# Hybrid encoder block on one core: the attention probabilities of two heads transposed in one step, with the products' PSUM bank as second target

## The chip, the cores and the metric

The kernel runs on one core of one Trainium2 chip. The time is the device time of one execution in microseconds (us). In the profile PE is TensorE, DVE VectorE, ACT ScalarE, POOL GpSimd and SP the engine that issues most of the DMAs; a head here is an attention head.

## The reference, cut to what matters

Two layers work on 256 tokens with 1024 channels in float32. A layer is a feed-forward half, a mixing half and a second feed-forward half. The mixing half projects the tokens once, runs two kinds of attention with eight heads each ("na" over a neighbourhood on a grid, "sw" over a sliding window with a learned sink), gates both and projects them back.

```python
for l in range(DEPTH):                                     # DEPTH = 2
    x = x + 0.5 * swiglu(rms_norm(x, ffn1_norm[l]), ...)
    z = rms_norm(x, mix_norm[l]) @ w_in[l]                 # q, k, v of both kinds, two gates
    o_na = neighbourhood_attention(qa, ka, va, na_rpb[l])  # 8 heads x 64
    o_sw = sliding_window_gqa(qs, ks_, vs, t5_bias, sw_sink[l])
    merged = g[:, :, 0] * (o_na @ w_branch_na[l]) + g[:, :, 1] * (o_sw @ w_branch_sw[l])
    x = x + merged @ w_out[l]
    x = x + 0.5 * swiglu(rms_norm(x, ffn2_norm[l]), ...)
# each kind of attention, for every head:
#   s = q k^T / 8 + bias (masked);  p = softmax(s);  o = p v
```

## The kernel before

Weights come through a ring of 512 KB pieces, and the float32 products are made of three fast matmuls: each operand is split into a rounded high part and a remainder, ScalarE writing the high part (line 184) and VectorE the remainder (line 185). For weights these are wh and wl, for probabilities ph and pl. Lines 170 to 172 are the three matmuls; one of them has 512 columns.

TensorE's order is the order of the program's text; the other engines' orders are set by a scheduler at build time that works with a modelled timeline, with a priority raised by 500 for the attention steps. Within the mixing half the heads' work is laid between the matmuls of the projections. A clock of the program (`now`, `tick`) counts 1 for three 512-column matmuls; `defer(lag, ...)` puts a step off until that clock has gone on by `lag`, and `need` calls it early where its result is wanted. A head goes through three such steps:

- `front(h)`: four matmuls make the scores (tile sc); VectorE adds the bias and finds the maximum (line 571); ScalarE takes the exponentials (line 574); VectorE sums and inverts (lines 579 and 580); GpSimd scales the rows (line 581). The rows are the tile S.
- `turn(h, S_)`, `P_LAG` = 10 after it (more for a few heads, by `MORE`): four transposes of 128x128 write the PSUM tile pt (line 589); ScalarE and VectorE split it into ph and pl.
- `back(h, ph, pl)`, `V_LAG` = 7.5 after that: four matmuls of 256 columns multiply the split probabilities with the values into one half of the PSUM tile po, which two heads share (line 603). ScalarE reads part of that half (line 607) and VectorE adds the rest (line 608) into the tile o; after the odd head o is split into oB (sw) or oA (na).

The tiles pt and po have one bank each, sc has two. S has `LAG` = 3 buffers, ph and pl have 2 each. The sixteen heads of a layer follow each other, first the eight of sw and then the eight of na; below they are called sw 0 to 7 and na 0 to 7. The gates (line 655) and the local and grid projections (lines 703 to 741) run beside the last heads.

Of the kernel before, what the change touches and what calls it, by code (L numbers as in the profile page):

```python
# [11 lines left out]
F32 = mybir.dt.float32  # L12
F32R = mybir.dt.float32r
# [8 lines left out]
P = 128  # L22
# [4 lines left out]
T = S // P  # L27
# [12 lines left out]
NEG = -1e30  # L40
RING = 6
RAW = 4
LAG = 3
H_LAG, NORM_LAG, QK_LAG, P_LAG, V_LAG, M_LAG = 7.9, 4.0, 16, 10, 7.5, 5.5
LAST_LAG = 6.1
MORE = {"Q1": 2, ("sw", 4): 1.5, ("na", 4): 2, ("na", 5): 1.5}
# [12 lines left out]
def hybrid_encoder(ctx, tc, x, w_gu1, w_d1, w_in, b_gate, qk_gain, rpb, sink, t5,  # L59
                   w_bna, w_bsw, w_out, w_gu2, w_d2, c_mask, c_band, out):  # L60
    nc = tc.nc
# [6 lines left out]
    ps_acc = ctx.enter_context(tc.tile_pool(name="ps_acc", bufs=1, space=PSUM))  # L68
# [19 lines left out]
    ident = const.tile([P, P], F32, name="ident")  # L88
# [35 lines left out]
    def linked(engine, emit):  # L124
        with ExitStack() as order:
            if engine in chain:
                order.enter_context(tc.issue_after(chain[engine].ins))
            inst = emit()
        if chain:
            chain[engine] = inst  # L130
        return inst
# [23 lines left out]
    def defer(lag, key, fn):  # L155
        later.append((now[0] + lag, len(later), key, fn))
        later.sort(key=lambda e: e[0])

    def need(*keys):
        for e in [e for e in later if e[2] in keys]:  # L160
            later.remove(e)
            e[3]()
# [16 lines left out]
    def flipped(ap):  # L179
        step, n = ap.ap[-1]  # L180
        return bass.AP(tensor=ap.tensor, offset=ap.offset + step * (n - 1), ap=[*ap.ap[:-1], [-step, n]])

    def split_to(hi, lo, src):
        linked("act", lambda: nc.scalar.activation(hi, src, AF.Copy))  # L184
        linked("dve", lambda: nc.vector.tensor_tensor(lo, src, hi.bitcast(F32), ALU.subtract))  # L185
# [301 lines left out]
    def mix(l, n, after):  # L487
        with tc.tile_pool(name="mix", bufs=1) as mp:
# [52 lines left out]
            def attend(name, ins, qT, kh, kl, kidx, bias_of, vcol, ready, oT, sink_l=None):  # L541
                oh, ol = oT
                po = [None, None]
                with tc.issue_after(rstd_done[0].ins):
                    bias = [bias_of(0), bias_of(1)]

                def urgent(fn):
                    def run(*args):
                        with tc.high_priority(500):
                            fn(*args)  # L550
                    return run

                @urgent
                def front(h):
                    need(*ins)
                    if h + 2 < NH:
                        bias.append(bias_of(h + 2))
                    b = bias.pop(0)
                    least = FMAX
                    if sink_l is not None:  # L560
                        sk, least = (v[:, sink_l * NH + h:sink_l * NH + h + 1] for v in (snk, nsnk))
                    ps = ps_acc.tile([P, T, S], F32, name="sc", tag="sc", bufs=2)
                    S_ = mp.tile([P, T, S], F32, name="S", tag="S", bufs=LAG)
                    mx = small.tile([P, T], F32, name="mx", tag="mx")
                    sm = small.tile([P, T], F32, name="sm", tag="sm")
                    for t in range(T):
                        for i, k in enumerate((kh, kl)):
                            nc.tensor.matmul(ps[:, t, :], qT[:, h, t * P:(t + 1) * P], k[:, kidx(h), :],  # L568
                                             start=i == 0, stop=i == 1)
                    for t in range(T):  # L570
                        nc.vector.tensor_tensor_reduce(S_[:, t, :], ps[:, t, :], b(t), -1.0, least,  # L571
                                                       ALU.add, ALU.min, mx[:, t:t + 1])
                    for t in range(T):
                        nc.scalar.activation(S_[:, t, :], S_[:, t, :], AF.Exp, bias=mx[:, t:t + 1], scale=-1.0,  # L574
                                             accum_out=sm[:, t:t + 1])
                    if sink_l is not None:
                        es = small.tile([P, T], F32, name="es", tag="es")
                        nc.scalar.activation(es, mx, AF.Exp, bias=sk)
                        nc.vector.tensor_tensor(sm, sm, es, ALU.add)
                    nc.vector.reciprocal(sm, sm)  # L580
                    nc.gpsimd.tensor_tensor(S_, S_, sm.unsqueeze(2).to_broadcast([P, T, S]), ALU.mult)  # L581
                    defer(P_LAG + MORE.get((name, h), 0), (name, h, 0), lambda: turn(h, S_))

                @urgent
                def turn(h, S_):
                    tp = ps_acc.tile([P, T, T, P], F32, name="pt", tag="pt")
                    for t in range(T):
                        for kt in range(T):
                            nc.tensor.transpose(tp[:, kt, t, :], S_[:, t, kt * P:(kt + 1) * P], ident)  # L589
                    ph = mp.tile([P, T, T, P], F32R, name="ph", tag="ph", bufs=2)  # L590
                    pl = mp.tile([P, T, T, P], F32R, name="pl", tag="pl", bufs=2)
                    split_to(ph, pl, tp)
                    defer(V_LAG, (name, h, 1), lambda: back(h, ph, pl))

                @urgent
                def back(h, ph, pl):
                    assert ready()
                    if h % 2 == 0:
                        po[0] = ps_acc.tile([P, 2, T, P], F32, name="po", tag="po")
                        po[1] = mp.tile([P, T, P], F32, name="o", tag="o", bufs=2)  # L600
                    for kt in range(T):
                        for i, p in enumerate((ph, pl)):
                            nc.tensor.matmul(po[0][:, h % 2], vcol(kt, h), p[:, kt], start=kt + i == 0,  # L603
                                             stop=kt + i == 2)
                    a, b = (0, DH) if h % 2 == 0 else (DH, 0)
                    o, ov = po[1], flipped(po[0][:, h % 2])
                    nc.scalar.activation(o[a:a + DH], ov[b:b + DH], AF.Copy)
                    nc.vector.tensor_tensor(o[a:a + DH], o[a:a + DH], ov[a:a + DH], ALU.add)
                    if h % 2:
                        split_to(oh[:, h // 2], ol[:, h // 2], o)  # L610

                for h in range(NH):
                    yield lambda h=h: front(h)
# [49 lines left out]
            def na_bias(h):  # L663
                t2 = mp.tile([P, T2W], F32, name="t2", tag="t2", bufs=2)
                for r in range(2):
# [10 lines left out]
                return lambda t: b[:, t].rearrange("p r c -> p (r c)")  # L676

            sw = attend("sw", ("Q0", "Q1", "K0", "K1"), sqT, *skT, lambda h: h // 4, sw_bias,
                        lambda kt, h: sv[:, kt, h // 4, h % 2 * DH:h % 2 * DH + P], lambda: True, oB, sink_l=l)
            na = attend("na", ("q0", "q1", "k0", "k1"), qT, *kT, lambda h: h, na_bias,  # L680
                        lambda kt, h: va[:, kt, h, :], lambda: "v1" in done, oA)
            step = {
# [8 lines left out]
            heads = iter([*[(sw, h) for h in range(NH)], *[(na, h) for h in range(NH)]])  # L691
            due = 0
            for token in ORDER.split():
                if token[0] == "a":
                    it, h = next(heads)
# [149 lines left out]
```

## Time and profile before

| | us |
|---|---|
| median of three runs (1076.62 to 1077.98) | 1076.77 |
| the profiled execution | 1076.94 |
| its span, first to last instruction | 1075.2 |

In the profile's groups, a row gives the line, the engine, the operation, what is written and read, how often, then the busy time in us and the mean of one in ns. In a list by time, a row gives the start and the length in us. The length of a matmul includes its way through the array, and matmuls overlap; what one costs is the distance from its start to the next start. The PE clock is TensorE's granted clock as a share of full speed; it was 0.999 over the span.

### The profile page before, as it was taken

Reading aid. Unit: us, or ns where it says so; the run is one execution under the profiler, and the core shown is the slowest. Engines: PE = TensorE matmul, PEld = TensorE weight load, DVE = VectorE, ACT = ScalarE, POOL = GpSimd, SP = SyncE. Lnnn points to the kernel's source line nnn. Section 1 sums busy time; section 2 is a strip of 40 time slices with the busy share of each in tenths; the row PEclk is TensorE's granted clock in tenths of the full one; section 3 lists DMA queues with packets and bytes.
Section 4 is the critical chain, followed back from the end, with each engine's and each line's share of the span. In section 5 each row is a group of like instructions: output and inputs, shape, how many; then the busy total and the mean of one; then the engine's idle time right before and its main releaser. Section 6 shows DMA issues by size and latency. Waiting matters only on the chain.

```text
span 1075.2 us, 14749 instructions
## 1 busy us (share of the span) xinstructions
PE 1068.2 (99%) x5125; PEld 890.3 (83%) x5125; DVE 875.8 (81%) x1337; ACT 671.5 (62%) x1014; POOL 116.7 (11%) x118
## 2 busy tenths in 40 slices
PE   8999999999999999999999999999999999999998
PEld 6888888888888888888888888888888888888887
DVE  6678799889886768869977887988898867778696
ACT  6566654788764556565565665557877646566552
POOL 1000120243520000000000000003534000000000
PEclk9999999999999999999999999999999999999999
DMA  7767656765654667756657765657666554776652
GB/s 247 227 214 237 215 190 191 228 194 155 192 188 137 198 199 246 242 168 191 214 162 238 227 213 185 199 153 247 177 195 185 176 175 160 237 231 203 188 196 89
DMA packets 98827, 212.63 MB, mean 198 GB/s; under 512 B 7568, under 2 KB 13744, under 8 KB 98752
## 3 DMA queue, kind: packets, MB, share of 16 engines
q1 hardware_dynamic: 98560, 211.60, 62.3%
q8 instruction: 40, 0.66, 0.2%
q14 instruction: 35, 0.29, 0.1%
q0 software_dynamic: 192, 0.08, 0.1%
HBM read 210.59 MB, written 1.06 MB: 197 GB/s over the span
## 4 chain that ended last, share of the span: by engine, by line
PE 97%; DMA 1%; ACT 1%; DVE 0%; issue 0%; SPq 0%; ACTq 0%
PE g L170 22%; PE g L172 22%; PE g L171 22%; PE acc L170 5%; PE acc L172 5%; PE acc L171 5%; PE tp L320 2%; PE sc L568 1%; PE po L603 1%; PE tp L170 1%; PE tp L171 1%; PE tp L172 1%; PE pt L589 1%; PE tp L201 1%; PE br L170 1%; PE br L171 1%
## 5 line engine op out<-in xcount | busy, mean ns | idle before, releaser
L185 DVE TENSOR_TENSOR wl<-raw,wh 128x1024 fp32r<-128x1024 f32 x336 | 405.7, 1219 | 65.5 <-ACT wh L184 61.8
L184 ACT ACTIVATE wh<-raw 128x1024 fp32r<-128x1024 f32 x336 | 346.7, 1045 | 117.3 <-DMA raw<-in_w_gu 51.4
L170 PE MATMUL g<-wh,xh 128*128 128x512 f32 (+1 forms) x976 | 383.1, 393 | 0.5 <-DVE hh L444 0.5
L172 PE MATMUL g<-wh,xl 128*128 128x512 f32 (+1 forms) x976 | 377.8, 387 | 0.0
L171 PE MATMUL g<-wl,xh 128*128 128x512 f32 (+1 forms) x976 | 377.5, 387 | 0.0
L172 PEld LDWEIGHTS g<-wh,xl 128*128 128x128 f32 x976 | 183.4, 188 | 39.1 <-DVE xl L185 1.5
L170 PEld LDWEIGHTS g<-wh,xh 128*128 128x128 f32 x976 | 183.6, 188 | 33.8 <-DVE hh L444 1.1
L171 PEld LDWEIGHTS g<-wl,xh 128*128 128x128 f32 x976 | 183.7, 188 | 33.4 <-DVE wl L185 0.6
L443 ACT ACTIVATE sg<-g,rs_y 128x256 f32<-128x256 f32 x88 | 41.1, 467 | 89.7 <-PE g L172 77.3
L444 DVE SCALAR_TENSOR_TENSOR hh<-g,rs_y,sg 128x256 f32<-128x256 f32 x88 | 42.3, 481 | 53.0 <-ACT sg L443 53.0
L170 PE MATMUL acc<-wh,hi 128*128 128x512 f32 x180 | 71.2, 395 | 0.0
L171 PE MATMUL acc<-wl,hi 128*128 128x512 f32 x180 | 70.2, 390 | 0.0
L172 PE MATMUL acc<-wh,lo 128*128 128x512 f32 x180 | 70.1, 390 | 0.0
L176 POOL TENSOR_TENSOR rs_y<-ms,mhalf 128x1 f32<-128x1 f32 x12 | 8.1, 678 | 556.5 <-DVE ms L222 548.0
L352 DVE TENSOR_TENSOR u<-raw 128x512 f32<-128x512 f32 x64 | 41.7, 686 | 20.9 <-DMA raw<-in_w_d 20.8
L184 ACT ACTIVATE corner<-raw 128x512 fp32r<-128x512 f32 x32 | 20.1, 629 | 40.4 <-DMA raw<-in_w_d 22.4
L581 POOL TENSOR_TENSOR S<-S,sm 128x512 f32<-128x512 f32 x32 | 37.2, 1161 | 65.6 <-DVE sm L580 38.3
L172 PEld LDWEIGHTS acc<-wh,lo 128*128 128x128 f32 x180 | 33.8, 188 | 7.2
L171 PEld LDWEIGHTS acc<-wl,hi 128*128 128x128 f32 x180 | 33.8, 188 | 6.7
L170 PEld LDWEIGHTS acc<-wh,hi 128*128 128x128 f32 x180 | 33.8, 188 | 6.7
L184 ACT ACTIVATE wh<-v 128x1024 fp32r<-128x1024 f32 x20 | 21.2, 1062 | 28.9 <-DVE v L352 24.5
L574 ACT ACTIVATE S<-S,mx 128x256 f32<-128x256 f32 x64 | 31.9, 499 | 8.0 <-DVE mx L571 7.9
(189 smaller groups left out, 1522.0 us busy)
## 6 DMA issues: line engine op xcount, KB each, us to landing
raw<-in_w_gu SPq DMA_DIRECT2D x176, 512.0 KB, 4.5
raw<-in_w_d SPq DMA_DIRECT2D x100, 512.0 KB, 4.2
raw<-in_w_in SPq DMA_DIRECT2D x64, 512.0 KB, 4.7
raw<-in_w_out SPq DMA_DIRECT2D x16, 512.0 KB, 3.6
bb<-in_b_gate SPq DMA_DIRECT2D x16, 256.0 KB, 3.6
raw<-in_w_bsw SPq DMA_DIRECT2D x8, 512.0 KB, 3.9
raw<-in_w_bna SPq DMA_DIRECT2D x8, 512.0 KB, 3.5
raw<-in_w_d SPq DMA_DIRECT2D x12, 256.0 KB, 2.7
```

The source lines that it names most:

```text
L170: nc.tensor.matmul(ps, xh, wh, start=first, stop=False)
L171: nc.tensor.matmul(ps, xh, wl, start=False, stop=False)
L172: nc.tensor.matmul(ps, xl, wh, start=False, stop=last)
L184: linked("act", lambda: nc.scalar.activation(hi, src, AF.Copy))
L185: linked("dve", lambda: nc.vector.tensor_tensor(lo, src, hi.bitcast(F32), ALU.subtract))
L201: nc.tensor.transpose(tp[:, i, :], xs[t][:, k * P:(k + 1) * P], ident)
L320: nc.tensor.transpose(tp[:, SLOT[t][i], :], hh[:, t, i * P:(i + 1) * P], ident)
L352: sub = lambda to, x, y: nc.vector.tensor_tensor(to, x, y, ALU.subtract)
L443: linked("act", lambda: nc.scalar.activation(sg, ps[:, :FC], AF.Silu, scale=rstd[t]))
L444: linked("dve", lambda: nc.vector.scalar_tensor_tensor(pair[0][:, t], ps[:, FC:], rstd[t], sg, op0=ALU.mult, op1=ALU.mult))
L574: nc.scalar.activation(S_[:, t, :], S_[:, t, :], AF.Exp, bias=mx[:, t:t + 1], scale=-1.0, accum_out=sm[:, t:t + 1])
L581: nc.gpsimd.tensor_tensor(S_, S_, sm.unsqueeze(2).to_broadcast([P, T, S]), ALU.mult)
```

## The change

Two heads are turned together. `front` keeps its head in a list, and only the odd head defers a turn, with its own lag. That turn transposes both heads: the even one into a tile with the tag po (the bank of the values' products), the odd one into pt. Both are then split, and one deferred step multiplies both with the values, the even head first. S has five buffers in place of three.

```diff
-LAG = 3
+LAG = 5
...
+                held = []
...
-                    defer(P_LAG + MORE.get((name, h), 0), (name, h, 0), lambda: turn(h, S_))
+                    held.append((h, S_))
+                    if h % 2:
+                        pair_, held[:] = list(held), []
+                        defer(P_LAG + MORE.get((name, h), 0), (name, h, 0), lambda: turn(pair_))
 
                 @urgent
-                def turn(h, S_):
-                    tp = ps_acc.tile([P, T, T, P], F32, name="pt", tag="pt")
-                    for t in range(T):
-                        for kt in range(T):
-                            nc.tensor.transpose(tp[:, kt, t, :], S_[:, t, kt * P:(kt + 1) * P], ident)
-                    ph = mp.tile([P, T, T, P], F32R, name="ph", tag="ph", bufs=2)
-                    pl = mp.tile([P, T, T, P], F32R, name="pl", tag="pl", bufs=2)
-                    split_to(ph, pl, tp)
-                    defer(V_LAG, (name, h, 1), lambda: back(h, ph, pl))
+                def turn(heads):
+                    tps = [ps_acc.tile([P, T, T, P], F32, name="pt", tag=tag) for tag in ("po", "pt")]
+                    for (_, S_), tp in zip(heads, tps):
+                        for t in range(T):
+                            for kt in range(T):
+                                nc.tensor.transpose(tp[:, kt, t, :], S_[:, t, kt * P:(kt + 1) * P], ident)
+                    ready_ = []
+                    for (h, _), tp in zip(heads, tps):
+                        ph = mp.tile([P, T, T, P], F32R, name="ph", tag="ph", bufs=2)
+                        pl = mp.tile([P, T, T, P], F32R, name="pl", tag="pl", bufs=2)
+                        split_to(ph, pl, tp)
+                        ready_.append((h, ph, pl))
+                    defer(V_LAG, (name, heads[1][0], 1), lambda: [back(*r) for r in ready_])
```

In the changed file the lines from `held = []` on have moved: the turn's transposes are line 594, the products line 611, ScalarE's and VectorE's reads of po lines 615 and 616, the scores line 569, the reductions 572, the exponentials 575 and the gates 663. In the orders below a row gives the line, the operation, the tiles and sizes, and in brackets the engines that it waits for; DVE is VectorE, Activation ScalarE and Pool GpSimd.

TensorE in layer 1, before: the products of head sw 3, six matmuls of a gate's projection, and the turn of head sw 5.

```order
L603 MATMUL po<-ph,sv 128x256 [waits DVE_49]
L603 MATMUL po<-pl,sv 128x256
L603 MATMUL po<-ph,sv 128x256
L603 MATMUL po<-pl,sv 128x256
L170 MATMUL g<-wh,xh_1793 128x512
L171 MATMUL g<-wl,xh_1793 128x512
L172 MATMUL g<-wh,xl_1794 128x512
L170 MATMUL g<-wh,xh_1793 128x512
L171 MATMUL g<-wl,xh_1793 128x512
L172 MATMUL g<-wh,xl_1794 128x512
L589 MATMUL pt<-ident,S 128x128 [waits DVE_49,PE_49,Pool_49]
L589 MATMUL pt<-ident,S 128x128
```

After, at the same place: the products of head sw 3 (those of sw 2 stand just ahead), six matmuls, and the turn of heads sw 4 and 5.

```order
L611 MATMUL po<-ph,sv 128x256 [waits DVE_49]
L611 MATMUL po<-pl,sv 128x256
L611 MATMUL po<-ph,sv 128x256
L611 MATMUL po<-pl,sv 128x256
L170 MATMUL g<-wh,xh_1793 128x512
L171 MATMUL g<-wl,xh_1793 128x512
L172 MATMUL g<-wh,xl_1794 128x512
L170 MATMUL g<-wh,xh_1793 128x512
L171 MATMUL g<-wl,xh_1793 128x512
L172 MATMUL g<-wh,xl_1794 128x512
L594 MATMUL pt<-ident,S 128x128 [waits DVE_49,Pool_49]
L594 MATMUL pt<-ident,S 128x128 x3
```

The products of two heads now stand together, and the first transposes behind them write the bank that these products wrote; the wait for VectorE there is for its last read of that bank. Before, it was for the remainder pl of the turn before.

ScalarE, after, around the products of heads sw 4 and 5: both reads of po (line 615) stand around the two exponentials of head na 0.

```order
L664 ACTIVATE gate_1821<-gate_1821 128x512 [waits DVE_49]
L615 ACTIVATE o<-po 64x256 [waits PE_49]
L575 ACTIVATE S,sm<-S,mx 128x256 [waits DVE_49,Pool_49]
L575 ACTIVATE S,sm<-S,mx 128x256 [waits DVE_49]
L615 ACTIVATE o<-po 64x256 [waits DVE_49,PE_49]
```

The second of the two reads waits for VectorE as well as for TensorE: VectorE's read of the even head's half comes first.

VectorE at the end of the attention stage, before: the reads of po for heads na 4 and na 5 (line 608) stand apart among the splits of the weights, two wl ahead of the first and two between them.

```order
L185 TENSOR_TENSOR wl<-raw,wh 128x1024 [waits DMAHW0_49,Activation_49]
L185 TENSOR_TENSOR wl<-raw,wh 128x1024 [waits DMAHW1_49,Activation_49]
L608 TENSOR_TENSOR o<-o,po 64x256 [waits Activation_49]
L185 TENSOR_TENSOR wl<-raw,wh 128x1024 [waits DMAHW2_49,Activation_49]
L185 TENSOR_TENSOR pl<-pt,ph 128x512 [waits Activation_49]
L655 SCALAR_TENSOR_TENSOR gate_1822<-g,rs_y,bb 128x512 [waits DMAHW5_49,PE_49]
L185 TENSOR_TENSOR wl<-raw,wh 128x1024 [waits DMAHW4_49,Activation_49]
L608 TENSOR_TENSOR o<-o,po 64x256 [waits Activation_49]
```

After, at the same place:

```order
L185 TENSOR_TENSOR wl<-raw,wh 128x1024 [waits DMAHW0_49,Activation_49]
L185 TENSOR_TENSOR wl<-raw,wh 128x1024 [waits DMAHW1_49,Activation_49]
L185 TENSOR_TENSOR wl<-raw,wh 128x1024 [waits DMAHW2_49,Activation_49]
L663 SCALAR_TENSOR_TENSOR gate_1822<-g,rs_y,bb 128x512 [waits DMAHW5_49,PE_49]
L185 TENSOR_TENSOR wl<-raw,wh 128x1024 [waits DMAHW4_49,Activation_49]
L616 TENSOR_TENSOR o<-o,po 64x256 [waits Activation_49] x2
```

Both reads now come behind all four wl and the gate; a split of probabilities has gone from between them, since both heads' splits stand earlier.

## The prediction

> **What bounds the kernel now.** I read the page first (busy shares), then the table by stretches over the two attention stages, then what TensorE waited for, and last the instructions in order of time around a few heads.
>
> ```profile
> span 1075.2 us, 14749 instructions
> PE 1068.2 (99%) x5125; PEld 890.3 (83%) x5125; DVE 875.8 (81%) x1337; ACT 671.5 (62%) x1014; POOL 116.7 (11%) x118
> ```
> ```profile
> core 0: us, PE busy (x) PEld busy (x) DVE busy (x) ACT busy (x) POOL busy (x), PEclk, DMA share, GB/s
> 224.00:325.00 101.00, 101.00 (x554) 86.06 (x553) 87.64 (x187) 78.65 (x167) 37.84 (x29) 1.00 0.61 184
> 755.00:856.00 101.00, 101.00 (x554) 86.05 (x553) 87.76 (x186) 78.63 (x168) 37.83 (x29) 1.00 0.61 184
> ```
> ```profile
> PE idle L120 <- DVE blank L115: 1.6, 1, 1.6
> PE tp L201 <- DMA x<-in_x: 1.3, 1, 1.3
> PE g L170 <- DVE hh L444: 0.5, 1, 0.5
> ```
>
> TensorE bounds it, and in the two attention stages (one a layer) it is busy for 101.00 of 101.00 us at full clock. Its only waits, 3.4 us, lie at the start and outside these stages. So an edit there gains only if TensorE's own instructions get cheaper, and every wait it brings TensorE is paid in full. VectorE, at 87.6 of 101, is the next tightest.
>
> **What TensorE pays for a turn.** The change issues the same transposes and products in larger groups. A group of four (a turn now) and a group of eight over two banks (the feed-forward's, line 320) both stand in the trace:
>
> ```profile
> 233.38 0.60 PE L589 MATMUL pt<-ident,S 128*128 128x128 f32 x4
> 233.73 0.48 PE L170 MATMUL g<-wh,xh 128*128 128x512 f32 x1
> 234.05 0.40 PE L171 MATMUL g<-wl,xh 128*128 128x512 f32 x1
> 234.28 0.39 PE L172 MATMUL g<-wh,xl 128*128 128x512 f32 x1
> ...
> 60.72 1.03 PE L320 MATMUL tp<-ident,hh 128*128 128x128 f32 x8
> ...
> 61.83 0.40 PE L171 MATMUL g<-wl,xh 128*128 128x512 f32 x1
> ```
>
> Starts count, since matmuls overlap. A plain 512-column matmul takes 0.23 us (234.05 to 234.28). Four transposes with the matmul behind them take 0.67 (233.38 to 234.05), so four cost 0.44. Eight take 1.11, so eight cost 0.88. Two groups of four cost as much as one of eight: the slow matmul behind a group is matched by the short step at its end. Joining turns saves 0.0. The bounds are 1.3 us saved (16 of 32 turns lose the 0.32 - 0.23 = 0.08 of their slow follower after all) and nothing lost.
>
> The products behave likewise, and this stretch also gives the distances:
>
> ```profile
> 259.19 0.72 PE L568 MATMUL sc<-skT,sqT 128*128 128x256 f32 x4
> ...
> 261.12 0.28 PE L603 MATMUL po<-ph,sv 128*128 128x256 f32 x1
> ...
> 261.47 0.28 PE L603 MATMUL po<-pl,sv 128*128 128x256 f32 x1
> 261.59 0.40 PE L170 MATMUL g<-wh,xh 128*128 128x512 f32 x1
> ...
> 262.99 0.60 PE L589 MATMUL pt<-ident,S 128*128 128x128 f32 x4
> ```
>
> Four products take 0.47 (261.12 to 261.59), 0.12 each, with nothing behind them. From the last product to the next turn it is 0.12 and six matmuls, 1.52 us. Before the change this distance costs nothing, since the turn writes bank pt and the products bank po.
>
> **The new wait.** Now the first four transposes of a pair write po, so they wait until both heads' products of the pair before have been read out of it: line 607 on ScalarE, line 608 on VectorE, for the even head and then for the odd one. In the new order the odd head's ScalarE read waits for the even head's VectorE read, so this is a chain of four. Every later instruction of TensorE stands behind the waiting transposes.
>
> A layer has eight pairs and seven such crossings. From the rows of the new order, at 0.23 a matmul, 0.12 a product and 0.11 a transpose, the last product stands ahead of the turn by 3.8, 1.5, 1.5, 3.4, 2.7, 2.7 and 1.5 us. When po is free follows from the work that stands ahead of the reads. F is the start of the last score matmuls (a front) before them.
>
> ```profile
> 262.15 1.22 DVE L185 TENSOR_TENSOR wl<-raw,wh 128x1024 fp32r<-128x1024 f32 x1 [0.61 <-ACT wh L184]
> ...
> 263.48 0.42 DVE L608 TENSOR_TENSOR o<-o,po 64x256 f32<-64x256 f32 x1
> ```
> ```profile
> 261.08 1.04 ACT L184 ACTIVATE wh<-raw 128x1024 fp32r<-128x1024 f32 x1
> ...
> 262.82 0.38 ACT L607 ACTIVATE o<-po 64x256 f32<-64x256 f32 x1
> ```
>
> *Second crossing* (heads sw 2, 3 to 4, 5). Ahead of the first read the new order has the same work: the front's reductions, an exponential, a weight piece's wh, the other exponential, then wl, then the read. With F = 259.19 that read ended at 263.90, F + 4.71. The odd head adds 0.38 + 0.42, and three hand-overs at 0.03 (wh ends at 262.12, wl starts at 262.15) add 0.09: F + 5.60. The turn stands four scores, twelve matmuls and eight products behind F, at F + 4.18. Wait: 1.42.
>
> ```profile
> 269.66 0.28 PE L568 MATMUL sc<-kh,qT 128*128 128x256 f32 x1
> ```
> ```profile
> 271.90 0.51 ACT L574 ACTIVATE S<-S,mx 128x256 f32<-128x256 f32 x1
> ...
> 272.41 0.49 ACT L574 ACTIVATE S<-S,mx 128x256 f32<-128x256 f32 x1
> ```
>
> *Third crossing* (sw 4, 5 to 6, 7). The order puts the new front's two exponentials between the two heads' reads. They ended at 272.90, F + 3.24 with F = 269.66; with 0.38 + 0.42 + 0.09 po is free at F + 4.13. The turn stands at F + 3.49. Wait: 0.64.
>
> ```profile
> 308.52 2.64 DVE L185 TENSOR_TENSOR wl<-raw,wh 128x1024 fp32r<-128x1024 f32 x2 [0.78 <-ACT wh L184]
> 311.08 0.40 DVE L608 TENSOR_TENSOR o<-o,po 64x256 f32<-64x256 f32 x1
> 311.42 1.21 DVE L185 TENSOR_TENSOR wl<-raw,wh 128x1024 fp32r<-128x1024 f32 x1
> 312.55 0.67 DVE L185 TENSOR_TENSOR pl<-pt,ph 128x512 fp32r<-128x512 f32 x1
> 313.15 0.73 DVE L655 SCALAR_TENSOR_TENSOR gate<-g,rs_y,bb 128x512 f32<-128x512 f32 x1
> 313.81 1.20 DVE L185 TENSOR_TENSOR wl<-raw,wh 128x1024 fp32r<-128x1024 f32 x1
> 315.04 0.42 DVE L608 TENSOR_TENSOR o<-o,po 64x256 f32<-64x256 f32 x1
> ```
> ```profile
> 310.81 0.60 ACT L184 ACTIVATE ph<-pt 128x512 fp32r<-128x512 f32 x1
> ```
> ```profile
> 304.63 0.28 PE L568 MATMUL sc<-kh,qT 128*128 128x256 f32 x1
> ```
>
> *Seventh crossing* (na 4, 5 to 6, 7). VectorE now takes three wl, the gate and a fourth wl ahead of both reads, where a read stood between them. With F = 304.63 the first wl started at F + 3.89; ScalarE has one more ph (0.60) ahead of it, so 4.48. Steps from start to start: 2.56 and 1.13 for three wl, 0.66 gate, 1.23 wl: the even read starts at F + 10.05 and ends at 10.45, and the odd pair with hand-overs frees po at about 11.3. The turn stands two groups of transposes and scores and thirty matmuls behind F, at F + 9.24. Wait: 2.0, rounded down, since fewer reads stand in between.
>
> ```profile
> 289.29 0.28 PE L568 MATMUL sc<-kh,qT 128*128 128x256 f32 x1
> ...
> 293.46 0.42 DVE L608 TENSOR_TENSOR o<-o,po 64x256 f32<-64x256 f32 x1
> ```
>
> *Fifth crossing.* By the same pattern as before the even read ends at F + 4.59, po is free at 5.48, the turn stands at 5.35: 0.13. Behind the last product the four lags are 2.9, 2.2, 3.5 and 2.8 us; the other crossings have 3.8, 3.4 and 2.7 us. I take 0 for them; at the longest lag, 3.5, they would cost 0.1 and 0.8.
>
> A layer pays 1.42 + 0.64 + 2.0 + 0.13 = 4.2, both layers 8.4.
>
> The Trainium skill's "PSUM — Partial Sum Buffer" (section on bank collisions) says that ScalarE and VectorE may not touch one bank and quadrant at once, even to read. The order's wait agrees with it; no run here shows a collision. Without it the odd ScalarE read could follow the even one at once and each wait would be about 0.4 shorter, 2.5 less in all over the three larger ones of each layer. "Perfetto Trace Analysis" (Matmuls) wants independent groups to rotate through banks, so that one's evacuation hides behind the next; by that, too, the change goes the wrong way.
>
> **The rest at nothing.** Of all heads this one's split ended latest behind its turn:
>
> ```profile
> 294.75 0.63 PE L589 MATMUL pt<-ident,S 128*128 128x128 f32 x4
> ...
> 299.48 0.68 DVE L185 TENSOR_TENSOR pl<-pt,ph 128x512 fp32r<-128x512 f32 x1
> ```
>
> That is 5.4 us (294.75 to 300.16). A pair's second split comes later than one alone by four transposes (0.44) and a ph (0.60), but its products stand 6.9 us or more behind the turn's start. Without that cover a late split would cost 0.5 each. Five buffers of S only hold the even heads longer; head 1's scaled rows are then wanted about when they were. No DMA is added; one load of gate biases and one scaling on GpSimd a layer move by a place.
>
> The profiled execution took 1076.94 us, 0.17 above the runs' median of 1076.77. 1076.94 + 8.4 = 1085.3.
>
> **Rivals.** *The bank is free in time.* The reads could come sooner if ScalarE and VectorE ran ahead of their rows; then nothing is left and the time is 1077. Against it: the bare chain, two reads each of 0.38 and 0.42, hardly fits 1.5 us. *Joining pays.* If the slow follower vanishes with each joined turn, 1.3 us go, 1075.6, still within 0.2% (2.15 us, about what can be told from no change). It turns into faster from 0.14 us a joined turn, 1074.7. The group of eight speaks against both. *Part of the waits.* The wl are done early in the last crossing and the odd reads overlap: 2 to 4 us, 1079 to 1081. *More waits.* The 2.7 us crossings wait too, or a second split is late: 4 us more, 1089. *The clock drops.* At the start, after idling, the matmuls ran at half pace:
>
> ```profile
> 1.60 2.50 PE L120 MATMUL idle<-blank 128*128 128x512 f32 x5 [1.60 <-DVE blank L115]
> ```
>
> The five take 2.50 us to the end of the last, nearly 0.5 each against 0.23. Were a 2 us wait in each layer to bring that back for some 3.5 us, half of it would be lost twice, 3.5 us: 1089. The Trainium skill's "TensorE: Matmul & The Clock Gate" (The HAM clock gate) lets the clock fall only after an idle window of about 3.4 us, longer than any wait that I forecast.
>
> **How the numbers follow.** Forecast 0.76 (its own range 1081 to 1087: down to 0.42 less at three crossings and another 1.0 less at the last, in each layer, 4.5 in all; up by the 0.9 a layer of the crossings that I took as free), part of the waits 0.09, more waits or the clock 0.05, free in time 0.07, joining pays 0.03 (0.02 of it beyond 0.2%). Slower is the first three less 0.01: 0.89. Same is 0.09, faster 0.02. The range 1079 to 1090 leaves out the last two and a little of the others, under 2 in 10.
>
> **What would show it.** TensorE's waits would name pt (line 594) behind VectorE's o (line 616), in the same places of both layers, about 1.4, 0.6 and 2.0 us; the attention stage would be some 4 us longer a layer, and groups of eight would cost 0.88. It is wrong if TensorE's busy share there stays whole, or if the waits name pl or S.

## The result: 4.2% slower, by waits inside a pair

The changed kernel takes 1123.04 us (median of four runs, 1116.92 to 1125.06) against 1077.25 (four runs, 1076.62 to 1077.98): a ratio of 1.0415, with an interval from 1.0399 to 1.0432. The forecast was 1085.3, with a range from 1079 to 1090. The profiled execution took 1124.55, its span is 1122.8, 47.6 more than before.

The page of the changed kernel, its span, busy shares and granted clock by slices:

```profile
span 1122.8 us, 14749 instructions
PE 1084.3 (97%) x5125; PEld 901.4 (80%) x5125; DVE 876.4 (78%) x1337; ACT 671.3 (60%) x1014; POOL 110.6 (10%) x118
...
PEclk9999999999989999999999999999899999999999
```

The instructions are as many as before, and VectorE's and ScalarE's busy times are unchanged. TensorE's share fell to 97%, and the clock has a dent in one slice of each attention stage. TensorE's waits, longest sum first (us in total, times, longest):

```profile
PE po L611 <- DVE o L616: 32.0, 16, 3.1
PE idle L120 <- DVE blank L115: 1.6, 1, 1.6
PE g L170 <- DVE hh L444: 0.5, 1, 0.5
...
```

The first row is new. It names po (line 611, the products) and not pt (line 594, the turn): the turn waits nowhere. Sixteen times, once a pair, products wait for VectorE's read of po. The table by stretches, same columns as in the prediction, for the first layer's attention stage:

```profile
224.00:345.00 121.00, 105.00 (x537) 88.91 (x536) 85.72 (x183) 76.51 (x164) 34.92 (x29) 0.94 0.48 149
```

Of 121.00 us 16.0 are idle, and a clock of 0.94 is some 7 more (0.06 x 121): together about 23 of the 23.8 us that each layer has become longer (half of 47.6). Now one pair in order of time, on TensorE, VectorE and ScalarE:

```profile
287.58 0.28 PE L611 MATMUL po<-pl,sv 128*128 128x256 f32 x1
290.56 0.38 PE L611 MATMUL po<-ph,sv 128*128 128x256 f32 x1 [2.71 <-DVE o L616]
290.79 0.28 PE L611 MATMUL po<-pl,sv 128*128 128x256 f32 x1
290.90 0.28 PE L611 MATMUL po<-ph,sv 128*128 128x256 f32 x1
291.02 0.28 PE L611 MATMUL po<-pl,sv 128*128 128x256 f32 x1
291.14 0.41 PE L170 MATMUL g<-wh,xh 128*128 128x512 f32 x1
```
```profile
287.04 3.14 DVE L185 TENSOR_TENSOR wl<-raw,wh 128x1024 fp32r<-128x1024 f32 x2 [0.26 <-ACT wh L184]
290.11 0.40 DVE L616 TENSOR_TENSOR o<-o,po 64x256 f32<-64x256 f32 x1
```
```profile
285.96 1.99 ACT L184 ACTIVATE wh<-raw 128x1024 fp32r<-128x1024 f32 x2
287.98 0.38 ACT L615 ACTIVATE o<-po 64x256 f32<-64x256 f32 x1
```

The even head's last product starts at 287.58. ScalarE reads po at once (287.98), but VectorE is in two weight remainders until 290.18 and ends its read at 290.51. The odd head's first product starts at 290.56. It writes the other half of the same bank, and in the program's order it stands behind the even head's reads of that bank. Before the change the products of a pair's two heads started 3.5 to 8.7 us apart in this layer. Head sw 3's started at 261.12, and VectorE's read of sw 2, the last of that half, had ended 2.5 us earlier:

```profile
258.25 0.40 DVE L608 TENSOR_TENSOR o<-o,po 64x256 f32<-64x256 f32 x1
```

The sum: 32.0 us of idle time, and 2.6 more that the starts show (34.6 from start to start beyond the usual 0.12, since each wait also lays bare 0.16 of the last product's way through the array, 0.28 - 0.12). The clock fell from 0.999 to 0.988 over the span, 0.011 x 1122.8 = 12.4, an estimate. Together 47.0 of 47.6.

**The clock.** The granted half clock comes in pieces of 3.41 us that start at 267.50, 291.39, 318.70 and 332.35 in layer 1: 7, 8 and 4 times 3.413 apart, so on a fixed grid. Stretches of that grid, two by two, of the changed kernel:

```profile
247.02:250.43 3.41, 1.73 (x10) 1.31 (x8) 3.41 (x8) 3.41 (x10) 0.00 (x0) 1.00 0.51 115
250.43:253.85 3.42, 2.03 (x14) 1.85 (x15) 1.84 (x6) 1.31 (x5) 2.04 (x2) 1.00 0.97 306
264.08:267.50 3.42, 1.50 (x9) 1.34 (x10) 2.00 (x5) 1.69 (x7) 1.04 (x1) 1.00 0.24 52
267.50:270.91 3.41, 3.41 (x16) 3.11 (x15) 2.36 (x4) 2.50 (x4) 0.00 (x0) 0.50 0.32 117
```

A wait of 3.1 us that was cut by the grid into 1.68 and 1.39 left the clock whole; one of 2.0 us that fell into one piece (1.92 idle of 3.42) brought half clock for the next.

### The profile page after: what moved, and what is told of

It reads as the page before. It is cut to its first block, busy times and chain, and to the rows that moved or that the text cites. A ratio compares the mean times of both kernels' runs of the same rounds, so it can differ in the third digit from the quotient of the medians.

```text
span 1122.8 us, 14749 instructions
## 1 busy us (share of the span) xinstructions
PE 1084.3 (97%) x5125; PEld 901.4 (80%) x5125; DVE 876.4 (78%) x1337; ACT 671.3 (60%) x1014; POOL 110.6 (10%) x118
## 4 chain that ended last, share of the span: by engine, by line
PE 77%; DVE 11%; DMA 4%; issue 4%; ACT 3%; SPq 0%; ACTq 0%; DVEq 0%
PE g L170 19%; PE g L172 19%; PE g L171 19%; DVE wl L185 5%; PE acc L170 3%; PE acc L172 3%; PE acc L171 3%; DMA raw<-in_w_d 2%; ACT wh L184 2%; PE tp L320 1%; PE po L611 1%; PE sc L569 1%; PE pt L594 1%; DVE u L352 1%; DVE v L352 1%
## 5 line engine op out<-in xcount | busy, mean ns | idle before, releaser
L582 POOL TENSOR_TENSOR S<-S,sm 128x512 f32<-128x512 f32 x32 | 34.1, 1071 | 69.5 <-DVE sm L581 50.0
```

## Experiments

The theory from this trace: the odd head's products wait for the even head's reads because they now follow at once in the same bank, and half clock is a result of these idle times. The rivals: the joined transposes, or po as their target, cost the time; without the wait inside the pair it would only move to the turn; the clock drops for another reason. Each version's rows have the lines of its own file: the products are line 607, 611 or 615, VectorE's read of po 612, 616, 617, 619 or 620, the turn 594 or 595.

**The products alone.** The kernel before, with single turns into pt as ever; only the products of two heads are joined (ph and pl get four buffers).

```diff
-                    defer(V_LAG, (name, h, 1), lambda: back(h, ph, pl))
+                    held.append((h, ph, pl))
+                    if h % 2:
+                        pair_, held[:] = list(held), []
+                        defer(V_LAG, (name, h, 1), lambda: [back(*r) for r in pair_])
```

> The kernel before with only the products joined: every head has its own turn into pt as before, the products of two heads stand together (even, its reads, odd, its reads), ph and pl have four buffers. No transpose writes po. Theory A: the odd head's products wait as in the changed kernel, 16 waits of 1 to 3 us, and the clock drops behind some: 1110 to 1125 us. Theory B: as before, 1077.

Measured: 1125.33 us, ratio 1.0447 [1.0431, 1.0463]. Its waits:

```profile
PE po L607 <- DVE o L612: 32.1, 16, 3.6
```

The same wait, as often and as long, with no joined transposes and none into po. The pairing of the products in one bank is enough for the whole loss.

**The reads last.** The changed kernel, with both heads' products first and then both heads' reads, which now stand in a step of their own, `take`.

```diff
-                    defer(V_LAG, (name, heads[1][0], 1), lambda: [back(*r) for r in ready_])
+                    defer(V_LAG, (name, heads[1][0], 1), lambda: [*[back(*r) for r in ready_], *[take(r[0]) for r in ready_]])
```

> The changed kernel with one edit: the products of both heads come first in the text, then the four reads of po, so no read of the bank stands between the two heads' products. Theory A (the odd head's products wait for the even head's reads, because both share one bank: 34.6 us, and the half clock that follows those waits: some 12 us): all of it goes, and what is left is the wait that the prediction had in mind, the turn's for the last read of po, 0.6 to 2.0 us at four crossings a layer: 1077 to 1086 us. Theory B (the time is lost because transposes and products share one bank, in whatever order): the waits only move to the turn, and the time stays at 1115 to 1125.

Measured: 1113.5 us, ratio 1.034 [1.0325, 1.0356]. The expected range was far too low. The eight products now follow each other 0.12 apart, but the waits went to the turn:

```profile
PE pt L594 <- DVE o L619: 22.9, 13, 3.1
PE br L170 <- ACT oA L184: 1.6, 2, 0.8
...
PE br L172 <- DVE oA L185: 1.1, 2, 0.6
```

VectorE between the two heads' reads, after the first pair's products (the last starts at 248.83; the next turn waits until 255.50):

```profile
251.21 0.41 DVE L619 TENSOR_TENSOR o<-o,po 64x256 f32<-64x256 f32 x1
251.54 0.47 DVE L539 SCALAR_TENSOR_TENSOR va<-g,rs_y,va 128x256 fp32r<-128x256 f32 x1
...
252.35 1.23 DVE L185 TENSOR_TENSOR wl<-raw,wh 128x1024 fp32r<-128x1024 f32 x1 [0.26 <-ACT wh L184]
253.49 1.40 DVE L532 SCALAR_TENSOR_TENSOR kl<-tp,qkg,kh 128x512 fp32r<-128x512 f32 x2
254.92 0.42 DVE L619 TENSOR_TENSOR o<-o,po 64x256 f32<-64x256 f32 x1
```

Between the two reads lie 3.3 us (251.62 to 254.92), nearly all of it other work that the order set at build time put there. So the rival held here: one bank for both heads and for the turn moves the wait rather than ends it.

**The reads last, and the products sooner.** The same with V_LAG 5 in place of 7.5, so that more matmuls stand between products and turn.

> As the run with the reads last, and the products stand 5 ticks behind the turn in place of 7.5, so the next turn comes 3.2 to 4.7 us behind the last product. Theory A: no wait of the turn is left, and joining the turns by itself neither costs nor saves: 1076 to 1079 us, unless a split is late for its products (0.5 us each). Theory B: over 1100. If joining eight transposes saved the slow matmul behind each turn: 1075.6.

Measured: 1093.01 us, ratio 1.015 [1.0135, 1.0165], clock 1.000. The larger rows of its waits:

```profile
PE pt L594 <- DVE o L619: 6.3, 6, 1.9
PE po L611 <- DVE pl L185: 3.8, 2, 1.9
```

The expectation missed again. The distance shortens the turn's wait, and it brings a late split of the probabilities: pl now ends up to 1.9 us after its products could start. Another 2.7 us go into waits for oA, as with the reads last.

**Two banks.** The changed kernel, with the odd head's products in pt, which its turn has left by then.

```diff
+                    po[0] = ps_acc.tile([P, 2, T, P], F32, name="po", tag=("po", "pt")[h % 2])
                     if h % 2 == 0:
-                        po[0] = ps_acc.tile([P, 2, T, P], F32, name="po", tag="po")
```

> The changed kernel with one edit: the even head's products go to the bank po, the odd head's to the bank pt, which its own split has left. Theory A (the odd head's products wait because the even head's reads are still due in the same bank): no wait between the two heads' products. The turn's waits for the reads stay, at the four crossings with 1.5 to 2.7 us from the last product to the turn. With the reads ending 0.9 to 3.0 us behind their head's products, as the changed kernel's trace has it, that is 0.5 to 1.5 us at about five crossings a layer: 1081 to 1092 us. Rival (products of two heads standing together are late for another reason, their own splits): waits on pl in place of those on the reads, 1100 or more.

Measured: 1083.09 us, ratio 1.0058 [1.0045, 1.0072], clock 0.999. As expected, 40 us of the loss are gone. What is left:

```profile
PE pt L594 <- DVE o L616: 3.9, 4, 1.2
...
PE pt L594 <- POOL b L683: 0.9, 2, 0.4
PE pt L594 <- POOL S L582: 0.8, 2, 0.4
```

These are waits of the kind that the prediction priced, the turn's for reads of the pair before. They are shorter by construction: the even head's transposes write po, where now only the even head's products were, and so wait for that head's reads alone. From start to start, in layer 1, they are 1.0 at the second crossing (forecast 1.42), 0.6 at the third (0.64), 0 at the fifth (0.13) and 1.2 at the seventh (2.0). The profile puts the third down to GpSimd's b:

```profile
273.43 0.41 DVE L616 TENSOR_TENSOR o<-o,po 64x256 f32<-64x256 f32 x1 [0.71 <-ACT o L615]
```
```profile
273.99 0.63 PE L594 MATMUL pt<-ident,S 128*128 128x128 f32 x4 [0.44 <-POOL b L683]
275.01 0.66 PE L594 MATMUL pt<-ident,S 128*128 128x128 f32 x4 [0.39 <-POOL S L582]
```

VectorE's read ends at 273.84, 0.15 before the turn, the same distance as at the second and the seventh crossing, so the read explains this wait as well. The odd head's transposes then wait for GpSimd's scaling of S, another 0.6 a layer from start to start, which the forecast had at nothing. The kernel is about 6 us slower than before. In this version the odd head's products also have a tile of their own; no run tells one bank apart from one tile.

**Two banks and lags.** First V_LAG 5.5 with two banks, then also a little more lag for two pairs whose splits were late.

> The same two banks, and the products 5.5 ticks behind the turn in place of 7.5, so that the turn comes 2.9 to 4.2 us behind the last product. Theory A, and joining the transposes neither costs nor saves by itself: all waits of the attention stages go but a few tenths, 1077 to 1081 us. If joining saved the slow matmul behind a turn: 1075.6. If the products are now too early for their splits (second splits 4 to 5 us behind the turn): 0.5 to 2 us a layer more.

Measured: 1083.48 us, ratio 1.0066 [1.0052, 1.008], no better than with the old lag. The turn's waits are gone, and late splits have replaced them, the expectation's case of products that come too early:

```profile
PE po L611 <- DVE pl L185: 3.4, 2, 1.7
```

```diff
+SOON = {("sw", 3): 0.5, ("na", 3): 2.5}
...
+                    defer(V_LAG + SOON.get((name, heads[1][0]), 0), (name, heads[1][0], 1), lambda: [back(*r) for r in ready_])
```

> The version with two banks and the products 5.5 ticks behind the turn, with half a tick more for sw 2 and 3 and 2.5 ticks more for na 2 and 3, where the run before waited 0.3 and 1.9 us a layer for a late split. Theory A, joining is worth nothing: the two waits go and no other comes, 1076.5 to 1079 us, within 0.2% of the kernel before or a little above. If joining saved the slow matmul behind a turn: 1075.5, at the edge of what can be told.

Measured: 1079.57 us, ratio 1.0027 [1.0017, 1.0038]; the waits left in the stage are

```profile
PE pt L595 <- DVE o L617: 1.6, 2, 0.8
```

That is a little more than expected. With nearly all waits gone the joined form comes near the time before and no lower. No version beat the kernel before.

**Buffers alone.** The kernel before with LAG = 5.

> The kernel before with five buffers of S in place of three and nothing else. All theories: TensorE has no wait that a buffer of S could take away, and the order of TensorE is the same: 1077, within 0.2%. A change would mean that the scheduler's order of the other engines, which the buffers also move, has a part in the 46 us.

Measured: 1076.84 us, ratio 1.0001 [0.9992, 1.0011]: no change.

**The wait filled.** The changed kernel, with nine matmuls of 512 columns, whose result nobody uses, between the two heads' products. Their target is a tile in pt's bank.

```diff
+                    else:
+                        fill = ps_acc.tile([P, 512], F32, name="fill", tag="pt")
+                        for _ in range(9):
+                            nc.tensor.matmul(fill, ident_r, ph.rearrange("p a b c -> p (a b c)"), start=True, stop=True)
```

> The changed kernel with nine idle matmuls of 512 columns (2.1 us at full clock, results not used) into pt between the two heads' products, where TensorE waits. Theory C (the half clock comes from TensorE's idling in these waits): the half clock goes, some 12 us less, while the shorter waits are filled up to 2.1 us, 4 us more: 1113 to 1119 us. Rival (the clock drops for another reason, such as the load or a throttle that is there anyway): half-speed matmuls stay, 1125 to 1132.

Measured: 1116.02 us (1115.64 to 1116.45), ratio 1.0362 [1.0344, 1.0379]. By its stretch and its waits:

```profile
224.00:345.00 121.00, 119.15 (x629) 100.01 (x628) 88.95 (x188) 79.17 (x168) 35.83 (x29) 1.00 0.51 154
```
```profile
PE po L615 <- DVE o L620: 3.7, 6, 1.0
```

TensorE does 144 matmuls more, 33.6 us at 0.233, and the kernel is 7.0 us faster than the changed one. The clock is 1.000: with waits of 1.0 us at most it does not drop. So the idle time brings the half clock, and the lost clock is a part of the price of its own.

**The wait partly filled.** The same with four matmuls.

> The changed kernel with four idle matmuls (0.93 us) between the two heads' products in place of nine. They fit into every wait (1.1 to 3.2 us), so the waits' own time stays as in the changed kernel, and only TensorE's idling is shorter, 0.1 to 2.3 us. Theory C (half clock after idling of over about 2.1 us): the clock stays up but for the longest wait, 1109 to 1114 us, that is the changed kernel less some 12. Rival (the clock follows the mean load, or anything but the length of the idling): half clock stays, 1119 to 1125.

Measured: 1113.4 us, ratio 1.0349 [1.0331, 1.0367], clock 0.998.

```profile
PE po L615 <- DVE o L620: 17.2, 12, 2.1
```

17.2 of idle time and 16 x 0.93 of filling are 32.1, the same waits as the 32.0 of the changed kernel, at 9.6 us less: most of what the clock alone had cost. Its attention stages hold only one piece of half clock, after 2.12 us of idle time that lie in one piece of the grid:

```profile
248.50:251.91 3.41, 1.29 (x7) 0.77 (x7) 3.29 (x10) 2.43 (x7) 0.44 (x1) 1.00 0.85 241
251.91:255.32 3.41, 3.41 (x14) 3.01 (x15) 0.91 (x2) 1.49 (x3) 1.60 (x2) 0.50 0.82 285
```

The same wait, 2.12 us, stands in layer 2, cut by the grid into 1.14 and 0.98, and there the clock stayed whole.

## Why the prediction was wrong

*What held.* TensorE bounds the stage and pays every wait in full: 32.0 of idle time came out as 34.6 of span. The joining itself is worth nothing: in the changed kernel eight transposes with the matmul behind them take 1.11 (239.90 to 241.01), so 0.88 as forecast, and the last two-bank kernel's span is 1077.3, 2.1 more than before, with 1.6 us of listed waits. The S buffers cost nothing. The change goes the wrong way, by readers of PSUM that are late, and the rule that the prediction drew on in the Trainium skill's "Perfetto Trace Analysis" (Matmuls), that independent groups should rotate through banks, pointed at this: rotating the two heads' products took 40 us off.

*The step that failed.* "The products behave likewise ... 0.12 each, with nothing behind them": that was measured on one head's four products and carried over to two heads' eight as if they followed each other. Between them lie the even head's two reads of the same bank, which the change leaves in the program ahead of the odd head's products. In the four shortest waits ScalarE starts as soon as the products are through and VectorE right behind it, and even these are 0.92 of idle time, 1.1 from start to start; sixteen of them alone would be 17 us. With exponentials and weight pieces queued ahead it was up to 3.2. The term was put at 0 and measured 34.6. The row stood in the order that was quoted, "L611 MATMUL po<-ph,sv 128x256 [waits DVE_49]", and it was there before the change too, where nothing was left to wait for. The prediction does not ask what of VectorE's that wait covers.

*The term that was priced.* The turn's wait was put at 8.4 and is 0: while the odd products wait, VectorE and ScalarE catch up, and the odd head's reads then follow each other at once, within the 1.5 us to the turn. The kind of wait was right: where the products do follow at once, the turn's waits come back. Their size was not shown. In one bank, with the reads last, they are 22.9 and not 8.4, in an order in which VectorE does other work between the reads; with two banks, where the even head's reads are enough, they are 6.5 us of span (1081.7 - 1075.2) with GpSimd's share. That 6.5 lies near 8.4 is in part luck. So the forecast priced the second queue behind the bank and missed the first.

*The clock.* Its drop was a rival with 0.05 for it and "more waits" together, at 3.5 us; it took 12.4. It was set aside with a sentence from the Trainium skill's "TensorE: Matmul & The Clock Gate" (The HAM clock gate), that the clock falls after an idle window of about 3.4 us. The window agrees with this trace in its length and its fixed grid (3.413), but it need not be wholly idle: 1.92 us idle in it were enough. With the waits at 2.0 or less that were forecast, the clock would have held nearly everywhere, as with two banks (0.999), where the longest was 1.2; with the waits that came, it did not.

## What to carry to other kernels

Work that is moved together is also moved past what stood between: for each PSUM bank list its writers and readers in program order, before and after, and ask of every wait in the order which reads and writes it covers, since a wait that cost nothing with 3.5 us or more of distance may cost its whole queue without it. Two accumulation groups that follow each other want two banks if the first is read before the second in the program. Where TensorE is the bound, price a wait of about 2 us or more with 1.7 us on top for each piece of half clock that it may bring.

## What was unexpected of the hardware

The clock is set piece by piece on a grid of 3.413 us. In the traces of the changed kernel, the products alone, the reads last and the four fillers, each piece with 1.92 us or more of idle time on TensorE was followed by half clock in the next, and none with 1.86 or less was, but for two named below, which stood at half clock themselves. The largest that went without, with the reads last, in layer 2:

```profile
853.81:857.22 3.41, 1.56 (x9) 1.04 (x7) 2.81 (x9) 3.11 (x7) 2.53 (x2) 1.00 0.49 154
857.22:860.63 3.41, 3.29 (x19) 2.88 (x20) 3.38 (x6) 2.31 (x6) 1.63 (x2) 1.00 0.54 167
```

So the same wait costs 0 or about 1.7 us by where it falls on the grid. That may be why the changed kernel's four runs, with clocks of 0.992, 0.991, 0.988 and 0.986, took 1116.92, 1121.53, 1124.55 and 1125.06, in that order; only the third has a trace, so it is not shown. Where between 1.86 and 1.92 the step lies, and why two pieces at half clock (the changed kernel's from 806.8, with 0.6 idle, and that of the products alone from 251.5, with 1.1) were followed by a second, stays open.
